# A third couple of up-projection groups, and the first parked chunk begun at group 8, in a two-layer encoder trunk

## The chip, the core and the metric

The kernel runs on one core of a Trainium2 chip. The core has a matrix engine (TensorE, called PE; its weight loads are shown as PEld), a vector engine (VectorE, DVE), a scalar engine (ScalarE, ACT), a general engine (GpSimd, POOL) and SyncE (SP), which here only issues transfers. Each engine works through its own instructions in order; the engines run beside each other and wait for one another through semaphores. The metric is the device time of one execution in microseconds (us); lower is better.

## The reference

The input is 256 tokens of width 2048 in float32. There are two layers; layer 0 mixes tokens with a gated MLP, layer 1 with latent attention. Each mixer is followed by a gated MLP with a short causal convolution, and every sublayer ends with `LayerNorm(ALPHA * x + sublayer(x))`. The change lies in the gated MLP, once a layer:

```python
def conv_ffn(x, w_up, conv_w, conv_b, w_down):
    h = x @ w_up                      
    h = causal_depthwise_conv3(h, conv_w) + conv_b
    a, g = jnp.split(h, 2, axis=-1)
    return (jax.nn.silu(g) * a) @ w_down   # 5504 -> 2048
```

The causal convolution is written out with `lax.conv_general_dilated` in the original; here it is shortened to its name.

## The kernel before

**Products in parts.** Each float32 operand is split into a high part (a cast by ACT, line 134) and a low part (what is left, a subtraction by DVE, line 137). A product is high times high, plus low times high, plus high times low. The activations are split once a layer (tiles `xhl`, four of them); the weights stream from memory in chunks of 128 x 2048 numbers (1 MB) and are split as they come.

**The feed.** `Feed` holds all weight chunks of the program in the order of use. `next` (called before PE works on a chunk) emits the loads some four chunks ahead and the splits two chunks ahead (more at a few places), then hands out the parts of the current chunk. Loads go on SP's queue into three raw slots. The split parts live in a pool of 14 slots of the tag "big", each 128 x 2048 numbers; a plain chunk takes two. The four `xhl` tiles, the two halves of the residual, and the activations `act` (one tile for each eight blocks) share the same 14 slots. A second tag, "side", has six slots of that size.

**Up projections, plain.** The 86 output blocks of `w_up` are worked in groups: group i computes two blocks of `a` and two of `g` for all 256 tokens, with the weights as the stationary operand (`plain`, `prod_a`). One plain group takes four chunks, and on PE 64 matmuls of 512 columns and 64 of 256. Its results have the tokens along the free dimension, as the convolution wants them. `pair` then adds the halves (`lo` and `h`, lines 409 and 411), runs the convolution (`c`, lines 1023 to 1026) and multiplies (`s`, `act`, lines 1040 and 1041).

**Up projections, coupled.** Two groups together form a couple (`summed`). There the tokens are the stationary operand, and four of the eight chunks (`UP_SEVEN`) are worked with seven products of blocks instead of eight, in the manner of Strassen and Winograd (`Banks.seven`). The weights' sums for this (`ts`, lines 144 and following in `_seven`) are made by DVE while the chunk is split, so such a chunk needs two high and two low parts (wh, wl, th, tl) and takes five slots for a while. The activations' sums are made once a layer by `combine_up`, for each of the four pairs of `UP_SEVEN`, into two shared rooms `xu`. A couple is 180 matmuls of 512 columns. Its outputs lie with tokens on the partitions; DVE finishes the sums (`rest`, lines 474 to 478, and line 1119), and PE turns them back with 16 transposes during the next plain group (`upr`, line 1049), in which the four `pair`s of the couple run too. Group 0 is part of the boundary between the sublayers. Before the change, the couples were (5, 6) and (8, 9); all others up to 21 were plain.

**What is slipped in between.** The table `EARLY` names work that is emitted after a chunk of a plain group: (group, chunk) -> what. `combine` is one of the four `combine_up`. `restore` f multiplies a quarter of the residual by the norm's gain and adds the bias, on both token halves (four DVE operations at lines 741 and 742, with two row loads on SP or POOL). `park` h stores half of the residual to memory by POOL's queue and frees its slot (line 718).

**Parked chunks.** Eight chunks of the down projection are prepared during the up projections by `park_all`, a generator that `plain` advances by one step at set places (`next(jobs, None)`). A first step loads a raw chunk by POOL (`look`, tile `praw`). Each chunk then has three steps in `Feed.park`: split three quarters of it (`pwh` by ACT, `pwl` by DVE, line 173) and store both; four additions (line 161), with the load of the next chunk; split the sums (`pth`, `ptl`) and store both. After each of the first six chunks comes one empty step; 31 steps in all. The tiles use "side" slots. The stored parts are fetched again when the down projection needs them.

**Order.** A scheduler orders each engine's instructions by the program's order and by when it takes them to be ready. `pin` (`keep_in_program_order`) keeps an instruction behind everything emitted before it on its engine; the steps of `park` and the first subtraction of each `combine` are pinned. `restore`, and the first addition of `combine_up`, are not.

Of the kernel before, what the change touches and what calls it, by code (L numbers as in the profile page):

```python
# [9 lines left out]
F32R = mybir.dt.float32r  # L10
# [5 lines left out]
P = 128  # L16
# [53 lines left out]
LEAD = 5  # L70
KEEP = {"wide": 4, "seven": 6, "parked": 6}

UP = [(1,), (2,), (3,), (4,), (5, 6), (7,), (8, 9), *((i,) for i in range(10, 22))]
UP_PAIRS = [0, 2, 1, 3, 5, 4, 6, 7]
UP_SEVEN = (2, 3, 4, 6)
EARLY = {(1, 2): ("restore", 0), (2, 1): ("combine", 0), (2, 2): ("restore", 1), (2, 3): ("park", 0),
         (3, 1): ("restore", 2), (3, 2): ("combine", 1), (3, 3): ("restore", 3), (4, 0): ("park", 1),
         (4, 1): ("combine", 2), (4, 2): ("combine", 3)}


def plan(n_k):

    return [[(int(t[:-1]), KINDS[t[-1]]) for t in line.split()] for line in PLAN[n_k]]


class Feed:
# [123 lines left out]
    def next(self, splits=2, loads=2):  # L210
        i = self.used
        self.ahead(i + 1 + splits + loads, i + 1 + splits)
        self.used += 1
        got = self.parts.pop(i)
        near = [j for j in range(i + 1, min(i + 1 + LEAD, len(self.chunks))) if self.chunks[j][2] == "parked"]
        if near and near[0] in self.kept:
            self.fetch(near[0])
        return got
# [3 lines left out]
def trunk(ctx: ExitStack, tc: tile.TileContext, x, xT, gm_in, gm_wout, ffn_up, ffn_dn,  # L222
# [12 lines left out]
    def slot(shape, name, dt=F32, tag="big"):  # L235
        return big.tile(shape, dt, tag=tag, name=name, bufs=SLOTS[tag])

    def bank(name):
        return ps.tile([P, 512], F32, tag="bank", name=name)
# [21 lines left out]
    for g in range(6):  # L261
        for p in U_PAIRS[g]:
            i = 48 + 8 * g + p // 2
# [15 lines left out]
    def up(w):  # L279

        for gis in ((0,), *UP):
            if len(gis) == 1:
# [36 lines left out]
    def combine(name, o, k1, k2):  # L319


        t = tp.tile([P, 4, P], F32, tag="t2", name=f"xs{name}", bufs=T2)
        turn(t, k1, k2)
        o = o.rearrange("p (h s c) -> p h s c", h=2, s=4)
        nc.scalar.copy(o[:, 0], t)
        nc.vector.tensor_tensor(o[:, 1], t, o[:, 0].bitcast(F32), ALU.subtract)
        return [(o[:, 0, i], o[:, 1, i]) for i in (1, 2, 0, 3)]
# [63 lines left out]
    def prod_a(acc, xs, ks, hi, lo):  # L391


        n = len(acc)
        w = lambda t, j, f: t[:, (j * n + f) * P : (j * n + f + 1) * P]
        turned = ks[0] // len(ks) % 2 == 1
        for wide in (False, True) if turned else (True, False):
            for j, k in enumerate(ks):
                x = xs[k // 4][:, k % 4, :]
                last = k == KD - 1 and wide == turned  # L400
                for f, a in enumerate(acc):
                    if wide:
                        mm(a, w(hi, j, f), x, k == 0, last)
                    else:
                        mm(a[:, 0:S], w(lo, j, f), x[:, 0:S], False, last)
# [624 lines left out]
    def ffn(layer, ln, acc, end, last):  # L1030
# [3 lines left out]
        def pair(a, acc_a, acc_g):  # L1034
            if act[a // 8] is None:
                act[a // 8] = slot([P, 8, S], f"act{layer}_{a // 8}", tag="side" if a // 8 in (0, 5) else "big")
            ca = conv(layer, a, acc_a, f"{layer}a{a}")
            cg = conv(layer, NF_FF + a, acc_g, f"{layer}g{a}")
            s = tp.tile([P, S], F32, tag="t1", name=f"s{layer}_{a}", bufs=T1)
            nc.scalar.activation(s, cg, AF.Silu)  # L1040
            nc.vector.tensor_tensor(act[a // 8][:, a % 8, :], s, ca, ALU.mult)
# [3 lines left out]
        def turn_back(t, src, b):  # L1045

            for f in range(4):
                o = (f % 2) * S + b * P
                nc.tensor.transpose(t[f // 2][:, o : o + P], src[:, f * P : (f + 1) * P], ident)

        def both(gi, t):

            for f in range(2):
                pair(2 * gi + f, t[0][:, f * S : (f + 1) * S], t[1][:, f * S : (f + 1) * S])

        def after(b, step, acc):
            if step == 0:
                ht[b] = tp.tile([P, 512], F32, tag="t2", name=f"upt{layer}_{b}", bufs=T2)
                nc.scalar.copy(ht[b], acc)
                return  # L1060
            if b == 0:
                hb.extend(bank(f"uph{layer}_{f}") for f in range(2))
            turn_back(hb, ht[b], b)
# [4 lines left out]
        sums, rooms = {}, []  # L1068

        def combine_up(p):  # L1070

            x = xhl[p // 2][:, p % 2 * 2 : p % 2 * 2 + 2]
            y = tp.tile([P, 2, S], F32, tag="t2", name=f"upy{layer}_{p}", bufs=T2)
            nc.vector.tensor_tensor(y, x[:, :, 0:S].bitcast(F32), x[:, :, S : 2 * S].bitcast(F32), ALU.add)
            if len(sums) % 2 == 0:
                rooms.append(slot([P, 2, 8 * P], f"xu{layer}_{p}", F32R))
            sums[p] = combine(f"u{layer}_{p}", rooms[-1][:, len(sums) % 2, :], y[:, 0], y[:, 1])

        early = {"restore": old.restore, "park": old.park, "combine": lambda i: combine_up(UP_SEVEN[i])}

        def plain(gi, turned):

            nt, nk = (4, 4) if gi < 21 else (2, 8)
            acc = [bank(f"up{layer}_{gi}_{f}") for f in range(nt)]
            for c in range(KD // nk):
                hi, lo = feed.next()
                prod_a(acc, xhl, range(nk * c, nk * c + nk), hi, lo)
                if c == 0 and turned:
                    for i, t in enumerate(turned[2]):
                        turn_back(turned[1][i % 2], t, i // 2)  # L1090
                if turned and 0 < c < 3:
                    both(turned[0][c - 1], turned[1][c - 1])
                if (gi > 9 and c > 0) or (gi, c) == (7, 3):
                    next(jobs, None)
                if (gi, c) in FIRST:
                    acts.make(*plan(NF_FF)[0][FIRST.index((gi, c))])
                if gi == 1 and c == 0:
                    after(1, 1, None)
                    both(0, hb)
                if (gi, c) in EARLY:  # L1100
                    name, i = EARLY[gi, c]
                    early[name](i)
            for f in range(nt // 2):
                pair(2 * gi + f, acc[f], acc[nt // 2 + f])
# [17 lines left out]
        turned = None  # L1122
        for gis in UP:
            if len(gis) == 2:
                turned = summed(gis)
            else:
                plain(gis[0], turned)
                turned = None
# [250 lines left out]
    for hf in range(2):  # L1379
# [13 lines left out]
        for b in range(2):  # L1393
            for f in range(2):
                c = slice(hf * 1024 + f * 512, hf * 1024 + (f + 1) * 512)
# [165 lines left out]
```

## Time and profile before

| | |
|---|---|
| time, median of 3 runs (lowest to highest) | 2449.04 us (2448.69 to 2449.54) |
| the profiled execution | 2449.38 us |
| its span, first to last instruction | 2447.3 us |
| its mean granted TensorE clock | 1.000 |
| up projections of layer 0, groups 1 to 21 | about 811 to 1263 us of the span |
| up projections of layer 1, groups 1 to 21 | about 1766 to 2218 us of the span |

The page gives for each engine its busy time and its share of the span. The chain of work that ended last is followed back from the last instruction: its shares say which engine set the end. Views by stage give the same busy times for a stretch of the span. A timeline row has start and length in us, engine, line, operation, tiles and shapes, and in brackets the idle time of the engine just before it and who ended it. A row of a group of instructions has the count, busy time in all and mean length of one in ns, then the idle time before them.

### The profile page before, as it was taken

How to read it: one execution, taken by the hardware profiler on the slowest of the kernel's cores; microseconds unless marked ns; L12 is line 12 of the kernel's file. 1: busy time of each engine (PE TensorE's matmuls, PEld its weight loads, DVE VectorE, ACT ScalarE, POOL GpSimd, SP SyncE). 2: the span in 40 equal slices, each digit the busy share in tenths (PEclk: the TensorE clock that was granted, in tenths of full speed). 3: DMA queues.
4: the chain of work that ended last, by engine and by line, in shares of the span. 5: the costliest groups of instructions: out<-in, count | busy, mean ns of one | idle time of the engine just before them, and what ended most of it. 6: DMA issues, size and time to landing. Idle time of an engine off the chain costs nothing.

```text
span 2447.3 us, 32249 instructions
## 1 busy us (share of the span) xinstructions
PE 2440.4 (100%) x12151; PEld 2065.3 (84%) x12151; DVE 2191.0 (90%) x2914; ACT 1512.4 (62%) x1997; POOL 140.6 (6%) x261
## 2 busy tenths in 40 slices
PE   9999999999999999999999999999999999999999
PEld 7888888888888888888888888988888888888887
DVE  7999999899998889998889897878798999888998
ACT  6666665566576655666665566665655666666553
POOL 0000000001010000011000000000000001010000
PEclk9999999999999999999999999999999999999999
DMA  7555666658796755799988885533575589898894
GB/s 293 203 205 205 233 202 205 207 173 304 254 296 241 239 205 194 258 359 374 341 318 320 320 298 172 188 141 126 207 272 184 181 323 375 321 371 300 314 353 178
DMA packets 128763, 627.37 MB, mean 256 GB/s; under 512 B 11592, under 2 KB 15184, under 8 KB 91616
## 3 DMA queue, kind: packets, MB, share of 16 engines
q1 hardware_dynamic: 94224, 462.47, 53.5%
q0 software_dynamic: 34384, 162.86, 17.9%
q8 instruction: 95, 1.56, 0.3%
q14 instruction: 60, 0.49, 0.1%
HBM read 552.35 MB, written 72.93 MB: 256 GB/s over the span
## 4 chain that ended last, share of the span: by engine, by line
PE 97%; DVE 1%; DMA 1%; ACT 0%; issue 0%; POOL 0%; ACTq 0%; DVEq 0%; POOLq 0%
PE up L242 30%; PE ub L242 16%; PE dn_q L242 8%; PE dn_p L242 6%; PE v_q L242 5%; PE v_p L242 4%; PE up_q L242 3%; PE up_p L242 3%; PE wo_q L242 2%; PE dn_e L242 2%; PE wo_p L242 2%; PE upf L242 2%; PE mo L242 2%; PE v_e L242 2%; PE mkv L242 1%; PE qn L242 1%
## 5 line engine op out<-in xcount | busy, mean ns | idle before, releaser
L137 DVE TENSOR_TENSOR wl<-raw,wh 128x1024 fp32r<-128x1024 f32 (+5 forms) x611 | 936.3, 1550 | 108.9 <-ACT wh L134 77.4
L134 ACT CAST wh<-raw 128x1024 fp32r<-128x1024 f32 (+5 forms) x611 | 790.9, 1318 | 307.2 <-PE up L242 67.8
L242 PE MATMUL up<-xhl,wh 128*128 128x512 f32 x2112 | 492.9, 390 | 0.0
L242 PEld LDWEIGHTS up<-xhl,wh 128*128 128x128 f32 x2112 | 392.3, 188 | 78.7
L134 ACT CAST th<-ts 128x1536 fp32r<-128x1536 f32 x196 | 203.7, 1051 | 173.9 <-DVE ts L144 144.2
L242 PEld LDWEIGHTS up<-xhl,wl 128*128 128x128 f32 x2112 | 262.4, 192 | 5.1
L242 PE MATMUL up<-xhl,wl 128*128 128x256 f32 x2112 | 265.1, 283 | 0.0
L137 DVE TENSOR_TENSOR tl<-ts,th 128x1536 fp32r<-128x1536 f32 x196 | 231.6, 1219 | 7.9 <-ACT th L134 3.3
L242 PE MATMUL ub<-wh,xhl 128*128 128x512 f32 x552 | 172.0, 393 | 0.0
L144 DVE TENSOR_TENSOR ts<-ts,raw 128x512 f32<-128x512 f32 x196 | 134.7, 687 | 2.0
L242 PEld LDWEIGHTS ub<-wh,xhl 128*128 128x128 f32 x552 | 103.6, 188 | 23.2 <-issue 1.9
L144 DVE TENSOR_TENSOR ts<-raw 128x1024 f32<-128x1024 f32 x98 | 119.5, 1219 | 2.2 <-DMA raw<-in_gm_in_dram 0.8
L242 PE MATMUL ub<-wl,xhl 128*128 128x512 f32 x276 | 107.5, 389 | 0.0
L242 PE MATMUL v_q<-wh,xhl 128*128 128x512 f32 x224 | 70.8, 391 | 0.0
L242 PEld LDWEIGHTS ub<-wl,xhl 128*128 128x128 f32 x276 | 51.8, 188 | 10.9
L242 PE MATMUL v_p<-wh,xhl 128*128 128x512 f32 x192 | 59.9, 389 | 0.0
L242 PEld LDWEIGHTS v_q<-wh,xhl 128*128 128x128 f32 x224 | 42.1, 188 | 9.7 <-ACT wh L134 0.9
L832 ACT ACTIVATE lny<-lnt,lncol 128x128 f32<-128x128 f32 x96 | 36.6, 471 | 15.7 <-PE lnt L828 15.6
L161 DVE TENSOR_TENSOR praw<-praw 128x512 f32<-128x512 f32 x64 | 43.9, 686 | 0.5
L242 PE MATMUL v_q<-wl,xhl 128*128 128x512 f32 x112 | 43.6, 389 | 0.0
L242 PE MATMUL mo<-wh,oT 128*128 128x512 f32 x128 | 42.7, 411 | 0.0
L242 PEld LDWEIGHTS v_p<-wh,xhl 128*128 128x128 f32 x192 | 36.0, 188 | 7.5
(2073 smaller groups left out, 4824.9 us busy)
## 6 DMA issues: line engine op xcount, KB each, us to landing
raw<-in_ffn_up_dram SPq DMA_DIRECT2D x172, 1024.0 KB, 5.9
raw<-in_gm_in_dram SPq DMA_DIRECT2D x93, 1024.0 KB, 5.3
raw<-in_ffn_dn_dram SPq DMA_DIRECT2D x68, 1024.0 KB, 7.7
raw<-in_gm_wout_dram SPq DMA_DIRECT2D x48, 1024.0 KB, 6.4
praw<-in_ffn_dn_dram POOLq DMA_DIRECT2D x16, 1024.0 KB, 12.5
keptth<-pth POOLq DMA_DIRECT2D x16, 1024.0 KB, 8.5
kepttl<-ptl POOLq DMA_DIRECT2D x16, 1024.0 KB, 8.7
fth<-keptth POOLq DMA_DIRECT2D x16, 1024.0 KB, 9.5
```

The lines of the kernel that those rows point to most:

```text
L134: cast = self.nc.scalar.copy(hi, raw)
L137: self.nc.vector.tensor_tensor(lo, raw, hi.bitcast(F32), ALU.subtract)
L144: add = lambda o, a, b: self.nc.vector.tensor_tensor(o, a, b, ALU.add)
L161: add = lambda o, a, b: pin(nc.vector.tensor_tensor(o, a, b, ALU.add))
L242: recent[0] = nc.tensor.matmul(o, l, r, start=start, stop=stop, skip_group_check=True)
L832: nc.scalar.activation(y[:, j], t[:, j * P : (j + 1) * P], AF.Identity, bias=lncol[:, o : o + 1], scale=lncol[:, g : g + 1])
```

## The change

A third couple is formed in each layer: the couples are now (3, 4), (6, 7) and (9, 10), with the plain groups 5 and 8 between them. All four combines are emitted in groups 1 and 2, and two of the four restores with the first park; the other two restores are emitted in groups 12 and 14, with the second park after the last. The two rooms of the activations' sums take "side" slots instead of "big" ones. The job that parks chunks takes its first step (a load) in group 5, the next two (first split, additions) in group 8, and goes on from group 11; before, it took the first in group 7 and went on from group 10.

```diff
-UP = [(1,), (2,), (3,), (4,), (5, 6), (7,), (8, 9), *((i,) for i in range(10, 22))]
+UP = [(1,), (2,), (3, 4), (5,), (6, 7), (8,), (9, 10), *((i,) for i in range(11, 22))]
...
-EARLY = {(1, 2): ("restore", 0), (2, 1): ("combine", 0), (2, 2): ("restore", 1), (2, 3): ("park", 0),
-         (3, 1): ("restore", 2), (3, 2): ("combine", 1), (3, 3): ("restore", 3), (4, 0): ("park", 1),
-         (4, 1): ("combine", 2), (4, 2): ("combine", 3)}
+EARLY = {(1, 1): ("restore", 0), (1, 2): ("combine", 0), (1, 3): ("combine", 1), (2, 0): ("restore", 1),
+         (2, 1): ("combine", 2), (2, 2): ("park", 0), (2, 3): ("combine", 3),
+         (12, 0): ("restore", 2), (14, 0): ("restore", 3), (14, 2): ("park", 1)}
...
             if len(sums) % 2 == 0:
-                rooms.append(slot([P, 2, 8 * P], f"xu{layer}_{p}", F32R))
+                rooms.append(slot([P, 2, 8 * P], f"xu{layer}_{p}", F32R, "side"))
...
-                if (gi > 9 and c > 0) or (gi, c) == (7, 3):
+                if (gi > 10 and c > 0) or (gi, c) in ((5, 3), (8, 2), (8, 3)):
                     next(jobs, None)
```

## The prediction, made before the changed kernel was run

> **What bounds the kernel now.** I read the page first: the busy shares and the chain of work that ended last.
>
> ```profile
> span 2447.3 us, 32249 instructions
> PE 2440.4 (100%) x12151; PEld 2065.3 (84%) x12151; DVE 2191.0 (90%) x2914; ACT 1512.4 (62%) x1997; POOL 140.6 (6%) x261
> PE 97%; DVE 1%; DMA 1%; ACT 0%; issue 0%; POOL 0%; ACTq 0%; DVEq 0%; POOLq 0%
> ```
>
> PE is the bound: 97% of the chain is its own work. So work removed from PE is time gained, as long as PE never waits for what feeds it. DVE stands second with 90%, as an average; the stages decide. Next I read the table of stages through the up projections of layer 0: two opening groups, two plain groups (3 and 4), the couple (5, 6), group 7, the couple (8, 9), then groups 10, 11, 12 and 14. The columns after the length are busy times and counts of PE, weight loads, DVE, ACT and POOL, then clock, DMA share and GB/s.
>
> ```profile
> 811.40:832.90 21.50, 21.50 (x129) 19.16 (x128) 17.14 (x25) 13.76 (x19) 0.00 (x0) 1.00 0.73 258
> 832.90:855.20 22.30, 22.30 (x130) 19.75 (x129) 21.25 (x36) 12.58 (x20) 0.55 (x1) 1.00 0.87 298
> ...
> 855.10:899.56 44.46, 44.46 (x258) 39.36 (x256) 38.99 (x68) 23.95 (x36) 1.26 (x2) 1.00 0.70 232
> 899.56:940.36 40.80, 40.80 (x182) 33.78 (x180) 37.04 (x42) 25.22 (x27) 0.00 (x0) 1.00 0.53 186
> 940.36:964.40 24.04, 24.04 (x146) 21.50 (x145) 22.48 (x36) 14.29 (x21) 0.00 (x0) 1.00 0.58 195
> 964.40:1005.50 41.10, 41.10 (x182) 33.56 (x181) 38.77 (x44) 24.56 (x27) 0.00 (x0) 1.00 0.55 189
> 1005.50:1029.60 24.10, 24.10 (x146) 21.56 (x145) 24.05 (x39) 17.39 (x26) 1.80 (x3) 1.00 0.75 263
> 1029.60:1051.80 22.20, 22.20 (x130) 19.66 (x129) 20.29 (x29) 13.17 (x17) 2.87 (x5) 1.00 0.98 362
> ...
> 1051.80:1074.10 22.30, 22.30 (x130) 19.75 (x129) 20.67 (x29) 13.75 (x20) 2.88 (x5) 1.00 1.01 420
> ...
> 1096.30:1118.50 22.20, 22.20 (x129) 19.66 (x129) 21.09 (x29) 15.19 (x20) 3.41 (x6) 1.00 1.01 391
> ```
>
> From the first couple to group 10 DVE is busy 22.48 of 24.04 us, 38.77 of 41.10, then 24.05 of 24.10: it has almost no room left, and the plain groups after that have 1 to 2 us each. The second couple is also 0.30 us longer than the first. The waits of the weight loads (us in total, times, longest) and the timelines of DVE and of the weight loads say why:
>
> ```profile
> PEld up_q L242 <- DVE tl L137: 0.8, 2, 0.4
> PEld up_p L242 <- DVE h_1a L411: 0.2, 1, 0.2
> PEld up_p L242 <- DVE h_0a L411: 0.2, 1, 0.2
> ```
> ```profile
> 964.25 0.42 DVE L411 TENSOR_TENSOR h_0a<-up,lo_0a 128x256 f32<-128x256 f32 x1 [0.76 <-ACT lo_0a L409]
> 964.59 2.35 DVE L137 TENSOR_TENSOR tl<-ts,th 128x1536 fp32r<-128x1536 f32 x2
> ...
> 969.47 0.48 DVE L1024 SCALAR_TENSOR_TENSOR c_0g<-h_0g,cst,c_0g 128x255 f32<-128x255 f32 x1 [1.40 <-ACT c_0g L1023]
> ...
> 979.93 1.76 DVE L137 TENSOR_TENSOR tl<-ts,th 128x1536 fp32r<-128x1536 f32 x1 [0.55 <-ACT th L134]
> ```
> ```profile
> 982.68 0.19 PEld L242 LDWEIGHTS up_q<-tl,xhl 128*128 128x128 f32 x1 [0.41 <-DVE tl L137]
> ```
>
> In the second couple, and in no other place of this phase, PE waits for DVE: for the low part of the sums of the fourth chunk (0.4 us) and for the banks that h (line 411) clears (0.2 us). The tl row counts two waits of 0.4, one a layer, and of the h rows one falls to each layer: about 0.6 us a layer. Here DVE already paces PE, with nothing to spare.
>
> **PE's gain.** Two plain groups cost 44.46 us (the stage of groups 3 and 4). A couple costs 40.80 us (the first, which has no wait) and turns its sums back with 16 transposes:
>
> ```profile
> 946.06 1.75 PE upr L1049 x16
> ```
>
> 40.80 + 1.75 = 42.55, so 1.91 us less for each new couple, one a layer: **3.8 us** off PE. If every wait went too (2 x 0.6), 5.0 us would be the most there is.
>
> **What DVE gets in return.** A cycle "plain group, couple" is 22.48 + 38.77 = 61.25 us of DVE in 65.14 us of PE (the rows of group 7 and the second couple); the 3.9 us between are waits inside its own chains (0.76, 1.40 and 0.55 are among them), which it cannot fill at will. After the change there are three couples in a row with only one plain group between, at 3-4, 6-7 and 9-10; I call them A, B and C.
>
> *A* starts two groups earlier, so the four combines and two of the four restores fall into groups 1 and 2. Their prices:
>
> ```profile
> L161 DVE TENSOR_TENSOR praw<-praw 128x512 f32<-128x512 f32 x32 | 21.9, 686 | 0.2
> L173 DVE TENSOR_TENSOR pwl<-praw,pwh 128x1536 fp32r<-128x1536 f32 x8 | 14.0, 1751 | 0.0
> L1074 DVE TENSOR_TENSOR upy<-xhl 128x512 f32<-128x512 f32 x4 | 2.7, 687 | 0.0
> L326 DVE TENSOR_TENSOR xu<-xsu,xu 128x512 fp32r<-128x512 f32 x4 | 2.7, 686 | 0.0
> L742 DVE TENSOR_TENSOR res<-res,lnp 128x512 f32<-128x512 f32 x4 | 2.7, 687 | 0.0
> L741 DVE TENSOR_TENSOR res<-res,lnp 128x512 f32<-128x512 f32 x4 | 2.6, 686 | 0.0
> L316 DVE TENSOR_TENSOR xsu<-xsu,upy 128x128 f32<-128x128 f32 x4 | 1.2, 289 | 0.1
> ```
>
> A combine is 0.69 + 4 x 0.29 + 0.69 = 2.5 us, a restore 4 x 0.69 = 2.7. Groups 1 and 2 had 17.14 + 21.25 = 38.4 us of DVE in 43.8, with one combine, the first step of a second (0.7) and three restores. They lose a restore (2.7) and gain what three combines still lack, 7.5 - 0.7 = 6.8: 42.5. The chunks prepared at their end are A's first two (about 2.3 and 6.8 us) where three plain ones (2.3 each) stood: +2.2, so 44.7. Of the 5.4 us that stood idle, 3.5 us lie at the opening, before the first convolutions, and I take them as not to be filled: 48 us for 43.8, or A's second chunk ready 4 us after A begins, 2.5 if instructions follow at 0.6 us where they last 0.69 (as below). In the old second couple that chunk was ready at 966.94, 2.5 us after its start at 964.40, and PE waited 0.6 us. So A's wait is 0.6 to 2.1; nine free slots of the big pool instead of seven (the rooms now stand in "side") may take 0.5 off: I take 0.8.
>
> *B* is the old cycle again: 0.6, with one slot more; I take 0.4 (bounds 0 and 1.3).
>
> *C* is the same cycle with the first parked chunk's first two steps in group 8: one split of 1.75 and four additions of 0.69, **4.5 us** by busy time. ACT's part (a cast) hides in ACT's 14.29 of 24.04. These steps are pinned in DVE's order, so what is queued behind them waits: the rest of C's second chunk, the h and c of group 8's convolutions (for which PE waits through the banks), and C's fourth chunk. What can take them in is DVE's idle time just there: 0.76 us (DVE will come too late to wait), perhaps the 1.40. 4.5 - 0.76 - 1.40 = 2.3 at best, 4.5 + 0.6 = 5.1 at worst; by start-to-start times (0.6 for an addition, 1.67 for the split: 4.1) and a slot that group 8 has more than group 7, 1 to 4. I take 2.1, nearer the lower end, since the old second couple shows DVE running without a break once it is late.
>
> The additions of a couple follow each other closer than they last:
>
> ```profile
> 1007.04 0.68 DVE L1119 TENSOR_TENSOR up_8w<-up_q,up_8w 128x512 f32<-128x512 f32 x1
> 1007.64 0.68 DVE L1119 TENSOR_TENSOR up_8p<-up_p,up_8p 128x512 f32<-128x512 f32 x1
> ```
>
> 0.60 us from start to start against 0.68. The Trainium skill ("VectorE: DVE Perf Modes", section "The DRAIN you can't avoid") says that after every operation the next waits until the pipeline is empty; these rows show starts 0.08 us before the end, and by the rule C's extra would be the 4.5 us instead of 4.1, 0.4 us more a layer.
>
> **The rest, at nothing.** Restores 2 and 3 go to groups 12 and 14 (2.7 us each; busy 20.67 and 21.09, where the job steps change by one place): over the room of 1.1 to 1.6 us, but the splits run two to three chunks of 5.6 us ahead; uncovered, 1 to 2 us. Their four row loads on SP and the residual's store on POOL come into groups with a DMA share of 1.01; behind them stand raw weight loads on SP and the parked stores on POOL, which a wait of theirs would hold: 0 to 2 us, and I take 0, since PE waits for no DMA there now. The load of the first parked chunk at group 5 takes a side slot and meets a DMA share of 0.58. The job's last step moves from group 19 to group 20, still ahead of the first fetch.
>
> **Sum.** A layer: -1.91 on PE, -0.6 for the old waits, +0.8 + 0.4 + 2.1 for the new: +0.8. Two layers: +1.6. The profiled execution took 2449.38 us (span 2447.3, 2.1 around it): 2451.0. The median is 0.34 lower: **2450.7**.
>
> **Rivals.**
> - *All hidden.* More slots and DVE's own idle time swallow the 4.5 us and A's opening: 2449.04 - 3.8 to - 5.0 = 2444.0 to 2445.2. For it: 3.9 us idle in a cycle. Against it: the 0.6 us of waits with less work. Chance 0.22, of it 0.05 over the bound.
> - *DVE becomes the bound of C.* The 4.5 us come on top in full, C waits 5.1 and A 2.1, B 0.6: 7.8 - 2.5 = +5.3 a layer, 2459.6; it decides as slower from waits of 5.0 us a layer on (net +2.5 x 2), with C at 3.8. For it: 24.05 of 24.10 in group 10, where these steps stand now. Against: those 24.05 cost PE nothing there. Chance 0.22, with a likely middle of 2456.
> - *A long wait costs clock as well.* All rows show a clock of 1.00 and no wait of PE over 0.41 us in this phase, so none shows what a wait of 3 to 4 us in C does. Were the next 3.4 us at half clock, each such wait would cost 1.7 us more, twice: 2459. The Trainium skill ("TensorE: Matmul & The Clock Gate", "Why this matters for your kernels") asks for no gaps over about 3 us between bursts, or the clock falls to half; no run here shows it. Chance 0.03.
> - *The late phase pays* (groups 12 to 20, DMA share 1.01): +1 to +2 a layer beside the forecast, 2453.5. Chance 0.05.
>
> **Chances.** Forecast 0.48. A run of this kernel can tell 0.2%, 4.9 us, from no change: faster 0.05, same 0.70, slower 0.25 (the two slower rivals). Range: from all hidden, 2444.4, to the middle of the second rival and a little over, 2457.5; outside lie its upper part and the best tip of the first, some 0.15.
>
> **What would show it.** Right: couples of 40.8 us plus 1.75; PE waits for tl or h in C of about 2 us, and DVE over 98% busy from group 2 on. Wrong: C free of waits (all hidden), or PE waiting on raw loads after group 11, or a clock under 1.00 in C.

## The result and the profile after

| | before | after |
|---|---|---|
| median of six runs each | 2449.48 us | 2463.52 us |
| lowest to highest | 2448.69 to 2450.43 | 2459.08 to 2467.80 |
| the profiled execution | 2449.38 us | 2467.80 us |

The changed kernel is slower: ratio 1.0055, 95% interval 1.0044 to 1.0066. The forecast was 2450.7 us with a range to 2457.5; the time lies 6 us above its upper end. After's runs also spread over 8.7 us, before's over 1.7.

The page of after, its head: the span, the busy times, and the granted clock of the core.

```profile
span 2466.0 us, 32043 instructions
PE 2446.6 (99%) x12031; PEld 2060.6 (84%) x12031; DVE 2223.0 (90%) x2938; ACT 1518.1 (62%) x1983; POOL 140.7 (6%) x261
```
```profile
core 0: 2466.0 us, clock 0.997
```

PE has the 120 matmuls less that the change promised (12151 before), and is nevertheless busy 6.2 us longer. The clock tells how that can be: before it was 1.000.

To see which stage lost the time I cut both traces at the first weight load of each stage (us; the last column ends with the span):

| | up to layer 0's up projections | up 0 | down 0 | layer 1's attention | up 1 | down 1 |
|---|---|---|---|---|---|---|
| before | 784.5 | 478.1 | 222.0 | 254.6 | 478.1 | 230.0 |
| after | 786.3 | 481.7 | 227.8 | 254.6 | 484.2 | 231.4 |
| difference | +1.8 | +3.6 | +5.8 | 0.0 | +6.1 | +1.4 |

Ahead of the up projections the program is unchanged. In the kernels run below that stage took 784.4 to 787.1 us, so its +1.8 is a difference between executions. The other 16.9 us are the change's: the up phases, which were to gain, lose 9.7, and 7.2 more are lost at the down projections, which the diff does not touch.

The table of stages for layer 0's up projections, with the same columns as before: couples A, B and C, and group 12.

```profile
856.70:897.60 40.90, 40.90 (x181) 33.58 (x180) 40.53 (x51) 25.75 (x30) 0.00 (x0) 1.00 0.61 204
...
921.60:962.90 41.30, 41.30 (x182) 33.62 (x181) 40.24 (x45) 26.13 (x29) 0.00 (x0) 1.00 0.57 187
...
986.80:1030.70 43.90, 42.01 (x182) 33.74 (x181) 40.63 (x48) 26.16 (x29) 1.84 (x3) 1.00 0.63 211
...
1054.70:1079.40 24.70, 22.61 (x130) 19.71 (x129) 24.70 (x41) 15.11 (x24) 2.63 (x5) 1.00 0.84 299
```

Couple A is about as long as the old first couple (40.90 against 40.80); B is 0.4 longer than A, C 3.0. Group 12 takes 24.70 us where a plain group took 22.2. The waits of the weight loads, over the whole kernel (us in total, times, longest; rows of waits that before had too are left out):

```profile
PEld up L242 <- issue: 5.1, 2, 2.6
PEld dn_p L242 <- DVE h_0a L411: 2.4, 1, 2.4
...
PEld up_p L242 <- DVE h_0a L411: 2.2, 3, 1.8
PEld up_p L242 <- DVE h_1a L411: 2.0, 2, 1.8
PEld up_q L242 <- ACT wh L134: 1.5, 2, 0.7
PEld dn_p L242 <- DVE h_1g L411: 1.4, 1, 1.4
PEld dn_p L242 <- DVE h_0g L411: 1.4, 1, 1.4
```

Rows up_p and up_q belong to the couples, row up (where the profile shows no releaser) to group 12, rows dn_p to the down projections. So there are **three places**, each in both layers: (a) couple C, (b) the start of group 12, (c) the start of the down projection. One at a time, with the engines that were late.

**(a) Couple C.** The timeline of the weight loads, then that of DVE just before:

```profile
997.41 0.30 PEld L242 LDWEIGHTS up_p<-th,xu 128*128 128x128 f32 x2 [1.79 <-DVE h_0a L411]
...
998.67 0.30 PEld L242 LDWEIGHTS up_q<-wh,xhl 128*128 128x128 f32 x2 [0.74 <-ACT wh L134]
...
1001.00 0.19 PEld L242 LDWEIGHTS up_q<-wl,xhl 128*128 128x128 f32 x1 [0.64 <-DVE wl L137]
```
```profile
989.20 1.76 DVE L173 TENSOR_TENSOR pwl<-praw,pwh 128x1536 fp32r<-128x1536 f32 x1 [0.94 <-ACT pwh L172]
...
994.29 0.68 DVE L161 TENSOR_TENSOR praw<-praw 128x512 f32<-128x512 f32 x1
...
996.94 0.42 DVE L411 TENSOR_TENSOR h_0a<-up,lo_0a 128x256 f32<-128x256 f32 x1
```

The first parked chunk's split (line 173) and its additions (line 161) stand between the operations of group 8's `pair`s, which end with the h at 996.94; that h clears the bank, and PE goes on at 997.41. The split even holds DVE idle for 0.94 us while it waits for its cast. Together 3.2 us in layer 0 and 2.5 in layer 1.

**(b) Group 12.** The weight loads stand for 2.48 us, up to 1058.49, and for 2.59 us in layer 1. PE waits for the last operations that read the couple's turned-back banks. ACT, DVE and PE, from their timelines:

```profile
1047.72 1.99 ACT L134 CAST wh<-raw 128x1024 fp32r<-128x1024 f32 x2 [3.87 <-DMA raw<-in_ffn_up_dram]
1049.62 0.41 ACT L1040 ACTIVATE s<-c_0g 128x256 f32<-128x256 f32 x1
```
```profile
1050.07 0.43 DVE L1041 TENSOR_TENSOR act<-s,c_0a 128x256 f32<-128x256 f32 x1 [3.47 <-ACT s L1040]
...
1057.90 0.47 DVE L1026 SCALAR_TENSOR_TENSOR c_0a<-upr,cst,c_0a 128x254 f32<-128x254 f32 x1
```
```profile
1058.52 2.32 PE L242 MATMUL up<-xhl,wh 128*128 128x512 f32 x9 [2.09 <-DVE c_0a L1026]
```

ACT stands 3.87 us at a cast whose raw chunk has not come; `s` is queued behind that cast, DVE stands 3.47 us for `s`, and the convolution for which PE waits ends at 1058.37. Two raw chunks issued beside the row loads of restores 2 and 3 took 9.0 and 9.2 us to land (9.4 and 10.3 in layer 1). SP's timeline shows these row loads in group 11, ahead of the place where the program emits them: the scheduler drew them forward. The DVE operations of these restores begin only at 1064.4 us (2029.5 in layer 1), after the wait; so of the restores only the row loads can have made it.

```profile
1032.28 0.33 SPq L738 DMA_DIRECT2D lnp<-in_ln_rows_dram  x1
...
1036.88 1.35 SPq L738 DMA_DIRECT2D lnp<-in_ln_rows_dram  x3
```

**(c) The down projection.** The weight loads, and ACT's casts ahead of them:

```profile
1279.19 0.30 PEld L242 LDWEIGHTS dn_p<-fth,dn01px 128*128 128x128 f32 x2 [2.42 <-DVE h_0a L411]
...
1281.12 0.50 PEld L242 LDWEIGHTS dn_p<-fth,dn01px 128*128 128x128 f32 x2 [1.40 <-DVE h_0g L411]
```
```profile
1263.01 1.91 ACT L134 CAST wh<-raw 128x2048 fp32r<-128x2048 f32 x1 [1.94 <-DMA raw<-in_ffn_dn_dram]
...
1269.55 1.91 ACT L134 CAST wh<-raw 128x2048 fp32r<-128x2048 f32 x1 [4.06 <-DMA raw<-in_ffn_dn_dram]
...
1278.25 0.35 ACT L409 COPY lo_0a<-up 128x256 f32<-128x256 f32 x1
```

Again ACT stands at casts for raw chunks, with the `lo` copies of the last groups' `pair`s queued behind; h comes late, and PE lacks its banks. The issues of transfers around the start of the down projection (KB each, median us to landing) of before and of after, and POOL's timeline of after:

```profile
raw<-in_ffn_dn_dram SPq DMA_DIRECT2D x7, 1024.0 KB, 7.4
```
```profile
raw<-in_ffn_dn_dram SPq DMA_DIRECT2D x6, 1024.0 KB, 12.1
```
```profile
1250.17 0.54 POOL L199 DMA_DIRECT2D fwh<-keptwh  x1
1252.91 0.53 POOL L166 DMA_DIRECT2D kepttl<-ptl  x1 [2.20 <-DVE ptl L173]
```

The job's last stores, issued at 1249.6 and 1252.9 us, now share the DMA engines with the first fetches of parked parts and with the raw chunks of the down projection. In before the last of these stores landed at 1241.5, ahead of its first raw chunk of the down projection (issued at 1244.4). The fetches stand among and behind these stores on POOL's queue, and come later too: the first was issued at 1250.2 us (1233.4 in before), and the four parts of the first parked chunk had landed at 1275.8 (1255.0). How much of the longer landings is due to the stores and how much to the later fetches, no run here separates.

**Clock.** Windows of the trace; the number after the five engines' busy times is the clock.

```profile
1276.60:1280.01 3.41, 1.42 (x6) 0.66 (x4) 3.41 (x7) 2.59 (x5) 0.37 (x1) 1.00 1.05 422
1280.01:1286.84 6.83, 5.87 (x15) 4.46 (x15) 6.83 (x11) 3.95 (x7) 1.06 (x2) 0.50 0.87 324
...
1959.27:1962.68 3.41, 1.73 (x8) 0.79 (x6) 1.53 (x5) 2.53 (x4) 0.00 (x0) 1.00 0.81 267
1962.68:1966.10 3.42, 3.42 (x8) 2.74 (x9) 3.42 (x5) 1.09 (x3) 0.00 (x0) 0.50 0.09 31
2020.71:2024.12 3.41, 1.22 (x6) 0.69 (x5) 3.41 (x8) 1.81 (x5) 0.00 (x0) 1.00 0.94 383
2024.12:2027.53 3.41, 3.41 (x10) 2.75 (x10) 3.41 (x5) 2.77 (x6) 1.25 (x2) 0.50 1.00 297
```

After (c) in layer 0, and after (a) and (b) in layer 1, PE ran at half clock: 6.83 + 3.41 + 3.41 = 13.65 us, in which it did the work of 6.8. So 6.8 of the 18.4 us are clock. After's six runs show the same: mean clocks of 1.000, 0.999 and 0.999 go with 2459.08, 2461.97 and 2459.35 us, and 0.998, 0.998 and 0.997 with 2465.07, 2466.22 and 2467.80.

### The profile page after: what moved, and what is told of

Same layout as the page of the kernel before. It is cut to its first block, busy times and chain, and to the rows that moved or that the text cites. A ratio compares the mean times of both kernels' runs of the same rounds, so it can differ in the third digit from the quotient of the medians.

```text
span 2466.0 us, 32043 instructions
## 1 busy us (share of the span) xinstructions
PE 2446.6 (99%) x12031; PEld 2060.6 (84%) x12031; DVE 2223.0 (90%) x2938; ACT 1518.1 (62%) x1983; POOL 140.7 (6%) x261
## 4 chain that ended last, share of the span: by engine, by line
PE 92%; DVE 3%; DMA 3%; ACT 1%; issue 1%; SPq 0%; ACTq 0%; DVEq 0%
PE up L242 23%; PE ub L242 16%; PE dn_q L242 8%; PE dn_p L242 7%; PE v_q L242 5%; PE up_q L242 4%; PE v_p L242 4%; PE up_p L242 3%; PE dn_e L242 2%; PE wo_q L242 2%; PE wo_p L242 2%; PE upf L242 2%; PE mo L242 2%; PE v_e L242 2%; DMA raw<-in_ffn_dn_dram 1%; DVE wl L137 1%
## 5 line engine op out<-in xcount | busy, mean ns | idle before, releaser
L137 DVE TENSOR_TENSOR wl<-raw,wh 128x1024 fp32r<-128x1024 f32 (+4 forms) x595 | 930.4, 1580 | 103.3 <-ACT wh L134 86.4
L134 ACT CAST wh<-raw 128x1024 fp32r<-128x1024 f32 (+4 forms) x595 | 786.0, 1342 | 300.4 <-DMA raw<-in_ffn_up_dram 93.3
L242 PE MATMUL up<-xhl,wh 128*128 128x512 f32 x1856 | 436.0, 391 | 4.3 <-DVE c_1a L1026 2.2
L242 PEld LDWEIGHTS up<-xhl,wh 128*128 128x128 f32 x1856 | 345.5, 188 | 74.3 <-issue 5.1
L137 DVE TENSOR_TENSOR tl<-ts,th 128x1536 fp32r<-128x1536 f32 x212 | 250.8, 1219 | 4.3 <-PE v_p L242 1.9
L242 PEld LDWEIGHTS up<-xhl,wl 128*128 128x128 f32 x1856 | 231.1, 192 | 4.6
L242 PE MATMUL up<-xhl,wl 128*128 128x256 f32 x1856 | 233.8, 283 | 0.0
L242 PE MATMUL up_q<-wh,xhl 128*128 128x512 f32 x192 | 60.6, 396 | 0.6 <-ACT wh L134 0.6
L242 PE MATMUL up_p<-wh,xhl 128*128 128x512 f32 x192 | 59.3, 392 | 0.0
L242 PEld LDWEIGHTS up_q<-wh,xhl 128*128 128x128 f32 x192 | 36.4, 190 | 8.9 <-ACT wh L134 1.5
```

The costliest lines, as they stand in the source:

```text
L134: cast = self.nc.scalar.copy(hi, raw)
L137: self.nc.vector.tensor_tensor(lo, raw, hi.bitcast(F32), ALU.subtract)
L242: recent[0] = nc.tensor.matmul(o, l, r, start=start, stop=stop, skip_group_check=True)
```

## The experiments

My theory after these readings: (a), (b) and (c) have three separate causes, in this order the job's two steps in group 8, the row loads of restores 2 and 3, and the place of the job's last step; the third couple itself pays. Rivals: one cause behind all (DVE is full, and what is taken from one place appears at the next); the couples themselves are too close for DVE; for (b) SP's queue, not the transfers. Each ratio is to runs of the kernel before on the same chip in the same session (medians 2450.08 to 2450.44), with its 95% interval. Where a time is set against after's 2463.52, that was measured in another session, whose median of before was 2449.48: 0.6 to 1.0 us less. The kernels of e8 and e9 leave out restores 2 and 3: they measure what these cost, and are no replacement for the kernel before.

| run | median us | ratio, interval |
|---|---|---|
| e1_late_restores | 2452.95 | 1.0013 (1.0004 to 1.0023) |
| e2_rows_on_pool | 2464.25 | 1.0057 (1.0042 to 1.0072) |
| e3_no_steps_in_8 | 2463.42 | 1.0055 (1.0040 to 1.0070) |
| e4_one_idle_less | 2457.32 | 1.0032 (1.0020 to 1.0044) |
| e5_rows_in_place | 2474.43 | 1.0100 (1.0086 to 1.0114) |
| e6_all_three_mended | 2466.63 | 1.0072 (1.0058 to 1.0085) |
| e7_c_alone | 2468.54 | 1.0077 (1.0063 to 1.0090) |
| e8_mended_no_late_restores | 2446.43 | 0.9984 (0.9974 to 0.9993) |
| e9_no_late_restores | 2459.95 | 1.0041 (1.0026 to 1.0056) |
| e10_restore_in_down | 2459.48 | 1.0036 (1.0023 to 1.0048) |
| e11_restore_in_5 | 2447.64 | 0.9989 (0.9980 to 0.9998) |
| e12_last_step_late | 2453.60 | 1.0013 (1.0003 to 1.0022) |

### Late restores alone, on the kernel before

```diff
-         (3, 1): ("restore", 2), (3, 2): ("combine", 1), (3, 3): ("restore", 3), (4, 0): ("park", 1),
-         (4, 1): ("combine", 2), (4, 2): ("combine", 3)}
+         (3, 2): ("combine", 1), (4, 1): ("combine", 2), (4, 2): ("combine", 3),
+         (12, 0): ("restore", 2), (14, 0): ("restore", 3), (14, 2): ("park", 1)}
```

> The kernel before, with one part of the change alone: restores 2 and 3 and the second park are emitted in groups 12 and 14. Theory (three separate causes: the job's steps in group 8 hold couple C; the restores' row loads, which the scheduler issues on SP's queue ahead of raw weight loads, hold group 11 and 12; the job's last step in group 20 holds the start of the down projection; each wait of 2 to 4 us also costs clock): the second cause alone is present, so PE waits 1 to 3 us a layer near the start of the group after the second couple's successor, none at the down projection; 2451 to 2457 us. Rival (DVE's sum of work is the cause and the waits are merely where its debt is collected): the early groups are relieved by 5 us of DVE a layer, nothing new waits; 2447 to 2450.

Measured: 2.9 us slower; the up phases are 479.3 and 479.2 us long instead of 478.1. The largest row of the waits of the weight loads, from the first couple to group 12 of layer 0:

```profile
PEld up_q L242 <- DVE wl L137: 1.4, 6, 0.3
```

No wait of 2.5 us at group 12, but a dozen in all of 0.1 to 0.3 us in the couples, where before had two rows of one wait each. A half of the residual that is parked at group 14 instead of group 4 keeps a slot through the couples, and their chunks are prepared with less lead; that the slot is the reason is argued from the place of the waits, and was not tried by itself. So late restores cost something here too, in another place than I thought. The row loads were drawn forward here too, into group 10, and two raw chunks beside them took 8.2 and 8.4 us to land, yet PE did not wait for it. ACT stood only 1.2 us for such a chunk (1.9 in layer 1), against 3.87 in after.

### The row loads on POOL's queue

```diff
-                (nc.gpsimd if self.idx == 1 else nc.sync).dma_start(t, src.to_broadcast([P, 512]))
+                (nc.gpsimd if self.idx == 1 or f > 1 else nc.sync).dma_start(t, src.to_broadcast([P, 512]))
```

> The changed kernel, with the row loads of restores 2 and 3 issued on POOL's queue instead of SP's. Theory: the wait of 2.6 us near the start of group 12 falls under 0.6 in both layers, couple C keeps its 3.2 and the start of the down projection its 1.4 to 3.8; 2453 to 2460 us, 4 to 8 less than the changed kernel on the same chip. Rival (DVE's debt): the wait stays at 2 us or more, or moves to the next groups; within 2 us of the changed kernel.

Measured: as after, within the intervals. The wait at group 12 is 0.45 us in layer 0 and still 2.53 in layer 1; the raw chunks beside the row loads took 8.0 and 9.2 us in layer 0, 9.0 and 9.3 in layer 1. The rival of SP's queue falls for layer 1: another queue does not bring the raw loads back to 5 us. PE's wait goes with ACT's: where ACT stood 2.84 us for the raw chunk (here, layer 0), PE waited 0.45; where it stood 3.87 to 4.96 (layer 1 here, and after), PE waited about 2.5; at 1.2 and 1.9 (the kernel before with late restores) not at all.

### No job steps in group 8

```diff
-                if (gi > 10 and c > 0) or (gi, c) in ((5, 3), (8, 2), (8, 3)):
+                if (gi > 10 and c > 0) or (gi, c) in ((5, 3),):
```

> The changed kernel, without the two job steps in group 8 (the load at group 5 stays, the first split comes at group 11, the last step two places later, in group 20). Theory: the waits in couple C fall from 3.2 us to 1.0 or less a layer; the start of the down projection gets worse by 1 us or more a layer, because the last step is later; in all 2455 to 2466. Rival (DVE's debt from three couples in a row): C still waits 2 us or more.

Measured: the same time as after, by a different way. Couple C of layer 0 has no idle time of PE any more (first row below, PE busy 43.50 of 43.50), so (a) is caused by these two steps. The up phases are 3.7 and 4.0 us shorter than after's. But every later step of the job now comes two places later, and (c) is 3.9 and 4.2 us instead of 3.8 and 1.4 (second fence, the waits: the longest of them, 3.4 in each layer):

```profile
985.50:1029.00 43.50, 43.50 (x193) 36.03 (x192) 40.36 (x49) 25.21 (x29) 0.00 (x0) 1.00 0.54 188
```
```profile
PEld dn_p L242 <- issue: 6.8, 2, 3.4
PEld up L242 <- ACT wh L134: 4.1, 2, 2.4
```

With its half clock the second down projection takes 236.0 us instead of 231.4. (b) remains, with 1.7 and 2.4 us (the row up).

### One empty step less: the last step in group 19

```diff
-            if n + 2 < len(todo):
+            if n + 3 < len(todo):
```

> The changed kernel, with one of the job's six empty steps left out (the one after the sixth parked chunk), so that its last step is in group 19 again, as before the change. Theory: the waits for h at the start of the down projection (3.8 us in layer 0, 1.4 in layer 1) fall under 0.5 each and the clock stays full there; 2454 to 2461. Rival (it is the volume of transfers, with the residual's store and the rows added behind group 11, and not the place of the last step): they stay at 1 us or more in at least one layer.

Measured: 6.2 us faster than after. The down projections are back at 222.3 and 230.0 us, with none of the dn_p waits; the raw loads in the same window as above take 7.9 us (7.4 in before), while (a) and some of (b), 0.9 and 1.9 us, remain:

```profile
raw<-in_ffn_dn_dram SPq DMA_DIRECT2D x6, 1024.0 KB, 7.9
```

So (c) is the place of the last step.

### The same from the other side: the last step late, on the kernel before

```diff
-                if (gi > 9 and c > 0) or (gi, c) == (7, 3):
+                if (gi > 9 and c > 0 and (gi, c) != (10, 1)) or (gi, c) == (7, 3):
```

> The kernel before, with the job's steps one place later from group 10 on, so that its last step is in group 20 as in the changed kernel; nothing else. Theory (the place of the last step alone): PE waits for h at the start of the down projection, 0.8 to 3.5 us a layer; 2451 to 2457. Rival (it needs the later loads of the residual and the rows too): no wait there over 0.5; 2448 to 2451.

Measured: 3.2 us slower. The up phases are unchanged (478.2 and 478.1), the down projections take 224.6 and 231.7 us, the raw loads at their start 11.0, and the two waits of (c) are there in both layers (the rows of 1.4, and 0.9 and 0.6 before them):

```profile
raw<-in_ffn_dn_dram SPq DMA_DIRECT2D x7, 1024.0 KB, 11.0
```
```profile
PEld dn_p L242 <- DVE h_1g L411: 1.4, 1, 1.4
PEld dn_p L242 <- DVE h_0g L411: 1.4, 1, 1.4
```

One place in the job's order, with nothing added, makes (c). No half clock follows in the profiled execution.

### Row loads held in their place

```diff
-                (nc.gpsimd if self.idx == 1 else nc.sync).dma_start(t, src.to_broadcast([P, 512]))
+                load = (nc.gpsimd if self.idx == 1 else nc.sync).dma_start(t, src.to_broadcast([P, 512]))
+                if self.idx != 1 and f > 1:
+                    behind(load)
```

`behind` makes a transfer start only after PE has reached the place where the program emits it.

> The changed kernel, with the row loads of restores 2 and 3 held in SP's order behind the matmuls of groups 12 and 14, where they are written. Which queue issues them has been seen not to matter. Theory (volume at one place: four row loads together beside two raw loads, which then take 9 to 10 us instead of 5, ACT stands on the raw load, and the convolutions that clear PE's banks stand behind it): the wait of 0.9 to 2.6 us near the start of group 12 falls under 0.5 in both layers, no raw load of group 11 takes over 7 us; the waits in C (3.3) and at the down projection (1.4 to 4) stay; up projections 1 to 2.5 us a layer shorter than in the changed kernel; 2454 to 2463. Rival (DVE's debt from three couples): the wait stays at 1 us or more.

Measured: 11 us slower than after. The wait at group 12 is gone in both layers (0.4 us stand in group 13 of one), as expected; but the rows now travel where the DMA share is about 1 (1.00 to 1.03 while they do), take 10 to 17 us to land, and DVE stands for them in order. DVE in group 14, and the waits of the weight loads:

```profile
1115.94 0.69 DVE L744 TENSOR_TENSOR sum<-sum,lnp 128x512 f32<-128x512 f32 x1 [1.82 <-DMA lnp<-in_ln_rows_dram]
```
```profile
PEld up L242 <- DVE wl L137: 13.5, 2, 7.7
```

The 1.82 us grow on their way: behind the row stands an h, ACT waits 2.98 us for it with the next chunk's cast behind, DVE can start that chunk's split at 1119.27 only, and PE has then stood for 5.9 us; some of it comes from before, when ACT stood 5.34 us for a raw chunk. In the other layer it is 7.7 us, and within each begin 6.83 us at half clock. So holding the row loads where they are emitted is no cure.

### All three mended at once, with the rows in place

```diff
-            if n + 2 < len(todo):
+            if n in (1, 3, 5):
...
-                if (gi > 10 and c > 0) or (gi, c) in ((5, 3), (8, 2), (8, 3)):
+                if (gi > 10 and c > 0) or (gi, c) in ((5, 3),):
```

This with the rows held as above; three empty steps fewer take up the two places given away in group 8.

> The third couple kept, and all three places mended: no job steps in group 8, three empty steps instead of six (the last step in group 19), the row loads in their place. Theory of three separate causes: waits of at most 0.6 us a layer in the up projections and none at the down projection; each layer's up projections take 476.3 to 477.2 us (478.1 before), clock full; 2445 to 2448 us, 2 to 4 less than before. Rival (three couples in a row bring a debt on DVE that is collected somewhere): new waits of 2 us or more a layer in groups 11 to 20, where the job is now denser; 2450 or more.

Measured: 2466.63, far from it. (a) is gone and of (c) 0.55 us are left in one layer, but the held rows make waits of 2.2 and 3.7 us in layer 0 and 2.1 and 5.2 in layer 1. It was my mending of (b) that failed, not the other two.

### Couple C alone

```diff
-            if n + 2 < len(todo):
+            if n + 3 < len(todo):
```

Again with the rows held; the steps in group 8 are kept.

> The row loads in place and the last job step in group 19, but the two job steps left in group 8: couple C's wait alone. Theory: 3.3 us a layer in C, up projections 479 to 480 us a layer without loss of clock; 2451 to 2457. Rival: within 1 us of the kernel with all three mended, since C's wait would be caught up later.

Measured: C waits 1.79 + 0.74 us in layer 0 and 1.79 + 0.74 + 0.64 in layer 1, the values of after with the layers exchanged. As a price for C alone the run fails, since the held rows make a wait of 9.6 us in layer 1.

### Without restores 2 and 3

```diff
-         (12, 0): ("restore", 2), (14, 0): ("restore", 3), (14, 2): ("park", 1)}
+         (14, 2): ("park", 1)}
```

> The changed kernel without restores 2 and 3: the gain and bias on one half of the residual are left out in both layers, with four row loads (1 MB) and eight DVE operations (5.4 us) a layer; everything else as changed. Theory (transfers and DVE work put into the job's stretch are what makes PE wait at group 12, and the last job step in group 20 what makes it wait at the down projection): the wait near the start of group 12 falls under 0.6; couple C keeps 3.2, the down projection keeps 1.4 or more in at least one layer; 2453 to 2460. Rival (three couples in a row and the dense job are enough): the wait near group 12 stays at 1.5 us or more.

Measured: 3.6 us faster than after. No wait at group 12 in either layer, and the raw chunks of group 11 land in 4.8 to 6.7 us: (b) comes from the restores, and by the times above from their row loads. (a) is still there, larger (1.38 + 2.45 + 0.34 in layer 0), for which I have no cause, and (c) with 0.9 us in layer 0, 0.8 + 1.4 in layer 1.

### The job mended, without restores 2 and 3

This is that kernel with the two edits of the job shown above for all three at once (steps in group 8 out, three empty steps fewer).

> As the kernel with all three places mended (no job steps in group 8, three empty steps instead of six), but restores 2 and 3 are left out instead of being held in place (gain and bias on one half of the residual missing). What is left of the change is the third couple with its combines. Theory: waits of at most 1 us a layer, up projections 476.3 to 477.5 us a layer, 2445 to 2448: the third couple pays its 1.9 us a layer as soon as nothing else is put beside it. Rival (debt of the third couple itself, with the job denser by a group): waits of 2 us or more a layer in groups 11 to 20, 2450 or more.

Measured: 2446.43, 3.8 us faster than before, and the clock is full in every run. The up phases take 476.7 and 476.4 us, 1.4 and 1.7 less than before. All three places are quiet; in the couples 1.1 us of waits a layer are left (one of 0.5, three of 0.2), where before had 0.6. Three couples are not too close for DVE by themselves. The rival of one cause behind all (DVE is full) is not settled by this run, which leaves out 5.4 us of DVE work a layer and its row loads; the second kernel of the next section puts them back.

```profile
core 0: 2444.2 us, clock 1.000
```

### Two other places for restores 2 and 3

The job is that of the kernel just above; its two edits, and the few lines that define `mend` and hand it over, are not shown again. First in the down projection, after its first fetch of the residual (half 1 is parked unrestored at group 1):

```diff
-         (12, 0): ("restore", 2), (14, 0): ("restore", 3), (14, 2): ("park", 1)}
+         (1, 0): ("park", 1)}
...
+                if mend and hf == 0 and i in (n - 5, n - 4):
+                    mend(ln, i - n + 7)
```

> The third couple with the job begun at group 11 and three empty steps (as in the mended kernels), the second half of the residual stored unrestored at the start, and restores 2 and 3 done in the down projection, after that half has been fetched again. Nothing is left out. Theory: the up projections keep 476.4 to 476.8 us a layer; the down projection has DVE idle enough for 5.4 us more, its stages grow by 0 to 2 us; 2445 to 2450, 0 to 5 less than before. Rival (DVE in the down projection is as full): waits of 2 us or more there, 2451 or more.

Measured: 2459.48. The up phases stay at 476.7 and 476.4 us, but DVE stands at the restore for its row, and PE waits behind it for 3.58 us in layer 0, 2.21 in layer 1, with smaller ones after; both are followed by half clock. DVE's timeline in the down projection of layer 0:

```profile
1359.54 1.29 DVE L743 TENSOR_TENSOR res<-res,lnp 128x512 f32<-128x512 f32 x2 [3.31 <-DMA lnp<-in_ln_rows_dram]
```

Second in group 5, with the park of that half in group 8:

```diff
-         (12, 0): ("restore", 2), (14, 0): ("restore", 3), (14, 2): ("park", 1)}
+         (5, 0): ("restore", 2), (5, 2): ("restore", 3), (8, 0): ("park", 1)}
```

> The same, with restores 2 and 3 in group 5 and the second park in group 8: 5.4 us of DVE between couples A and B instead of in the job's stretch. Theory (couples leave DVE no room for work beside them, as the job's 4.5 us in group 8 showed): couple B waits 2 to 5 us a layer, C 0.5, none later; 2450 to 2458. Rival (DVE's total up to group 21 counts, not the place): waits under 1 us, 2445 to 2448.

Measured: **2447.64 us, ratio 0.9989 (0.9980 to 0.9998)**, 2.8 us less than before and 15.9 less than after; the gain over before is small, but its interval ends below 1. The wait of 2 to 5 us that I expected in B did not come. The page of this kernel, and the windows that were group 5, couple B and couple C in after (here each stage begins some 1.4 us earlier, or more):

```profile
span 2446.3 us, 32039 instructions
PE 2437.8 (100%) x12031; PEld 2057.2 (84%) x12031; DVE 2221.3 (91%) x2938; ACT 1516.6 (62%) x1983; POOL 140.3 (6%) x261
```
```profile
897.60:921.60 24.00, 24.00 (x146) 21.46 (x145) 22.19 (x38) 11.56 (x19) 0.58 (x1) 1.00 0.71 234
921.60:962.90 41.30, 40.86 (x178) 32.99 (x177) 41.00 (x47) 26.43 (x30) 0.00 (x0) 1.00 0.58 195
...
986.80:1030.70 43.90, 43.90 (x196) 36.35 (x195) 40.76 (x50) 25.46 (x29) 0.00 (x0) 1.00 0.53 186
```

The rows come at a DMA share of 0.71, C has no idle time of PE, and 5.4 us of DVE work (two restores) cost PE about 0.6 us a layer beside the kernel without them (477.3 and 477.1 against 476.7 and 476.4). With DVE's work back in full (2221.3 us busy, after 2223.0) the three places stay quiet, and so the rival of one cause behind all falls. The 4.5 us of the job's steps in group 8 cost 2.5 to 3.2. One difference that fits: restores are not pinned, so the scheduler can put them where DVE is idle, while the job's steps stand where they are emitted, between the operations that clear PE's banks. That pinning is the reason was not tried by itself; the restores also stand ahead of another couple, and none of them waits for a cast.

## Why the prediction failed

- **PE's gain** (1.91 us a layer): held. With all three places quiet the up phases became 1.4 and 1.7 us shorter, while the couples' waits were 1.1 us a layer instead of 0.6: -1.91 + 0.5 = -1.4.
- **A** (0.8): 0.4, two waits of 0.2 in each layer. The 3.5 us of opening that I took as not to be filled, or the slots, made up more than I gave them.
- **B** (0.4): 0.43.
- **C** (2.1, bounds 1 to 5.1): the mechanism was right, down to h and the banks (no steps in group 8, no waits); the size is 3.2 and 2.5 us. I had priced DVE's time and left out that the pinned split itself waits 0.94 us for its cast. The 0.64 us between the layers go with the clock: of the ten couples C with both the steps and the restores (after, e2, e4, e5 and e7, two layers each), the five with half clock right behind the first waits lack this third wait, the other five have it.
- **"The rest, at nothing": the step that failed.** Two parts of it failed. For the restores' row loads I wrote "0 to 2 us, and I take 0, since PE waits for no DMA there now"; they gave (b), 2.5 and 2.6 us of waits. Taking these restores out made the kernel 3.6 us faster. "PE waits for no DMA" was true and no argument: ACT works in order, so a raw chunk that is late by some us holds `s` and `lo`, these hold DVE, and DVE holds PE's banks. I had also placed the loads at groups 12 and 14, where they are emitted, while they ran in group 11. For the job's last step I wrote "still ahead of the first fetch" and took nothing. By order of issue that was not so (the first fetch went out at 1250.2 us, the last store at 1252.9), and what counted were the transfers beside the raw chunks of the down projection. That place alone costs 3.2 us on the kernel before, and moving it back took 6.2 us off after, where its waits are 5.2 us instead of 4.3 and carry half clock in layer 0.
- **The clock rival** had 0.03, and "no run here shows it" was the reason. It came in three of six places of the profiled execution, 6.8 us. It stood for one wait of 3 to 4 us in C; what happened were waits of 1.8 to 2.6 us. It was a surcharge on every other rival and should have been priced with each.
- **The late phase** was the right place with the wrong chance (0.05) and size (+1 to +2 a layer without clock).

How it adds up for the profiled execution: the waits of (a), (b) and (c) are 5.7 (3.2 and 2.5), 5.1 and 5.2 us, together 16.0; those of A and B are 0.3 us a layer above the old ones. The couples' gain takes 3.8 off, half clock adds 6.8: +19.6 for a measured +16.9 behind the start. Some 0.6 are counted twice, since 1.1 us of the 1.40 in front of 1281.12 lie inside the half-clock stretch. The rest is not traced in full: the weight loads run ahead of the matmuls, so their waits overstate PE's (2.48 against 2.09 at group 12). By PE's own idle time, as modelled, the same stages have 11.4 us more than before, and the sum is +14.4, too little.

The effects do not add between kernels: taking the steps out of group 8 gained nothing alone (it pushed the job's end later), and with the other two mended it belongs to a kernel that is 15.9 us faster than after. What stays open: why C waits longer without the late restores, whether pinning is what makes the job's steps dearer than the restores, and whether at the down projection it is the job's stores or the later fetches that hold the raw chunks.

## What to carry to other kernels

Work that is "off the path" is only so together with its transfers: before moving a load or a store, look at the DMA share where it will run, and at which in-order engine will stand at the transfers that it slows. When a job is shifted, look at where it ends, not only at where it begins. And when a stall of about 2 us can cost clock as well, price it with that surcharge.

## What the runs showed of the hardware

**Half clock without a 3 us gap.** In all nine kernels here that had such stretches ahead of their last microseconds, they begin at whole multiples of 3.4133 us from one another (in after the second and third begin 200.0 and 218.0 windows behind the first) and last one, two or three windows. This agrees with the Trainium skill ("TensorE: Matmul & The Clock Gate", "What's actually happening"), which gives a free-running window of 3413 ns. The rule of thumb of that page of the Trainium skill ("Why this matters for your kernels"), no gaps over about 3 us, is too lax for this kernel: 1.80 + 0.74 us of waits in couple C sufficed (the row 1959.27:1962.68 above, with PE idle for 1.68 of 3.41 us), as did a wait of 2.21 us. By the modelled ends of the matmuls PE was idle for 0.49 or more of the window ahead of each of the 21 stretches; the windows with less (up to 0.45) were never followed by one. Three windows with 0.50, 0.51 and 0.52 were not either; after's is this one, with PE idle for 1.71 us:

```profile
1054.73:1058.14 3.41, 1.70 (x8) 1.08 (x6) 3.41 (x8) 2.51 (x5) 0.80 (x2) 1.00 0.95 387
```

So about half a window of idle time decides here, without a sharp edge, and where the waits fall against the windows differs from run to run; the spread of after's six runs goes with the granted clock.

**Small loads slow large ones.** Four row loads of 256 KB each, beside raw loads of 1 MB, went with landings of 9.0 to 10.3 us for two of these, against 4.8 to 6.7 in the same place in the kernel without the row loads; issued by POOL instead of SP it was 8.0 to 9.3. Where the DMA share was about 1, the row loads themselves took 10 to 17 us.
